# Output projection and first feed-forward blocks of a hybrid GDN layer: earlier row loads, operand preparation in parts, a deferred last tile

## The chip, the cores and the metric

The kernel runs on one core of a Trainium2 chip. The metric is device time in microseconds (us) of one execution, as the median of several runs. Before the change the median of three runs is 2518.31 us (2517.99 to 2518.65). A smaller number is better.

## The reference, cut to what matters

One layer is computed for a prompt of 2048 rows and 128 sample rows, 2176 rows in all, with a width of 1024 and a feed-forward width of 2816 (22 blocks of 128). The change touches the last two lines only:

```
h   = rmsnorm(x);  P = h @ w_in                    # q, k, v, gates, short convolution
o   = gated delta rule(q, k, v, ...);  y = short gated convolution(...)
mix = concat([o, y]) @ w_o
x   = x + rmsnorm(mix, norm_mix_post)
h   = rmsnorm(x, norm_ffn_pre)
x   = x + rmsnorm((silu(h @ w_gate) * (h @ w_up)) @ w_down, norm_ffn_post)
```

## The kernel before, in words

The 2176 rows are 17 tiles of 128 rows, numbered 0 to 16. Every fp32 matrix is split in a high and a low part ("h" and "l" in names such as `xh`, `xl`, `woh`, `wol`), and each product is made of three: high by high, high by low, low by high. The high part is a cast on ScalarE, the low part a subtraction on VectorE or GpSimd.

The program has these stages, by their time in the profiled execution: the projection by `w_in` with convolution and delta rule (0 to about 905 us), the output projection (905 to 1115 us), gate and up products (to about 2010 us) and the down products (to the end). The change lies at the second stage and at its border to the third.

**Output projection.** `o_tile(t)` (line 1022) handles one tile. `o_load` (line 1007) loads the mixer's rows `mr` in two halves (one buffer) and the residual row tile `xo` (two buffers) on SP's queue. `mix_split` (line 983) makes `mh` and `ml` of each half. TensorE then does 48 matmuls of 128x512 (line 1031): 24 for each half of the rows, alternating between two PSUM banks, `dbank` (a pool of 3) and `tbank` (a pool of 2), which hold the two halves of the columns. Behind them stands a chain: squares of the two banks on ScalarE (L1035), their sum on VectorE (`oss`, L1036), the inverse root (`oxm` on VectorE L145, `oxr` by a power on GpSimd L147), scaling on VectorE (L1040), the add into `xo` (L1041), a store to `x2d` on ScalarE's queue, squares of the new rows on ScalarE (L1044), their sum (`oss` L1045), a second inverse root (`oym`, `oyr`), the scaled rows `hx` (L1048, one VectorE instruction of 128x1024), 8 transposes on TensorE into two `ftbank` banks (a pool of 3, L1054), two VectorE multiplications to `ht` (L1055), and a store to `hTd` on ScalarE's queue. `xo` of tile t+2 needs the buffer of tile t, so its load waits for `hx` of tile t.

**Preparing the feed-forward rows.** The feed-forward stage takes the tiles in groups; group 0 holds tiles 0 to 5. Its products follow a Strassen-Winograd scheme of 7 products per block. Seven operands ("parts", in the order B11, T3, T1, T2, B21, T4, B22) are made of blocks of the transposed rows, four column pieces (k = 0 to 3) each: `ffn_load` (line 1141) reads 8 pieces `fh` back from `hTd`, `ffn_sums` (line 1152) makes T3 and T1 on VectorE (L1158, L1159), `ffn_prep` (line 1168) makes T2 (L1175), T4 (L1177) and, for all seven parts, the high cast on ScalarE (L1181) and the low subtraction (L1182), on GpSimd for k = 0 and on VectorE for the others. All that is issued in program order ahead of tiles 8 to 14: with `O_SPLIT` 8, one part ahead of each of the tiles.

**Gate and up blocks.** Block f of a group does seven products of 12 matmuls of 128x384 (L1254) in four PSUM banks (`fbank`, from the same 8 banks in turn: pool `psd` with 3, `pst` with 2, `pft` with 3, and over again). `gu_weights` (line 1203) loads the block's weights `rg` and `ru`, makes four sums (`sA` to `sD`, L1220 to L1223) on VectorE, and splits seven operands `fw`. `gate_up` (line 1277) issues the last three products, fetches the weights of the next block (`ffetch`) and does the elementwise part (`u` L1296, `m` L1297, `c` L1301 to L1303, and so on). Before the first block, weights are fetched and, at its end, the pool for later groups' rows is opened.

**What sets the order.** The program is written as a sequence, and when the kernel is built a scheduler with a modelled timeline puts the instructions of each engine in the order in which they will run. On the chip each engine runs its list in that order. `tc.issue_after(i)` holds what is issued inside it until instruction i is placed.

Of the kernel before, what the change touches and what calls it, by code (L numbers as in the profile page):

```python
# [9 lines left out]
F32 = mybir.dt.float32  # L10
# [3 lines left out]
ALU = mybir.AluOpType  # L14
# [27 lines left out]
        3: (6, 12, 15, 22, 17, 27, 31, 47, (51, 54, 57, 59), 61),  # L42
        4: (6, 12, 15, 20, 17, 24, 29, 42, (45, 48, 50, 52), 55)}
TLS = True
O_SPLIT = 8
NPD, NPT, NPG = 3, 2, 2
NR, NKV, NACC = 3, 2, 3
XKB = 4
# [36 lines left out]
def kernel(  # L85
# [72 lines left out]
    with ExitStack() as ph:  # L158
# [824 lines left out]
        def mix_split(v):  # L983
            mh = oa.tile([P, KD // 2, P], F32R, tag="mh", name="mh", bufs=3)
            ml = oa.tile([P, KD // 2, P], F32R, tag="ml", name="ml", bufs=3)
            A.copy(mh, v)
            V.tensor_sub(ml, v, mh.bitcast(F32))
            return mh, ml
# [28 lines left out]
            nc.sync.dma_start(out=xt, in_=x[t])  # L1017
            return mr, xt

        ahead = []  # L1020

        def o_tile(t):
            mr, xt = ahead.pop() if ahead else o_load(t)
            pss = [psd.tile([P, 512], F32, tag="d", name="dbank"), tbank()]
            for kh in range(2):
                mh, ml = mix_split(mr[kh]) if t else ready_m[kh]
                for j in range(4):
                    k = 4 * kh + j
                    for ci, (m_, w_) in enumerate(((mh, woh), (mh, wol), (ml, woh))):
                        for n in range(2):  # L1030
                            T.matmul(pss[n], m_[:, j, :], w_[k][:, n * 512:(n + 1) * 512],
                                     start=(k == 0 and ci == 0), stop=(k == KD - 1 and ci == 2))
            ss = op.tile([P, 4], F32, tag="oss", name="oss", bufs=2)
            for n in range(2):
                A.activation(ojunk, pss[n], AF.Square, accum_out=ss[:, n:n + 1])  # L1035
            V.tensor_add(ss[:, 0:1], ss[:, 0:1], ss[:, 1:2])  # L1036
            r = rstd(op, ss[:, 0:1], 1, 1.0 / D, EPS, "ox")
            for n in range(2):
                c = slice(n * 512, (n + 1) * 512)
                V.scalar_tensor_tensor(pss[n], pss[n], r, gpost[:, c], op0=ALU.mult, op1=ALU.mult)  # L1040
                V.tensor_add(xt[:, c], xt[:, c], pss[n])  # L1041
            nc.scalar.dma_start(out=x2d[t], in_=xt)
            for n in range(2):
                A.activation(ojunk, xt[:, n * 512:(n + 1) * 512], AF.Square, accum_out=ss[:, 2 + n:3 + n])  # L1044
# [3 lines left out]
            V.tensor_scalar_mul(hx, xt, r)  # L1048
            ht = op.tile([P, KD, P], F32, tag="ht", name="ht") if t else spare[1]
            for n in range(2):  # L1050
                ps = pft.tile([P, 512], F32, tag="t", name="ftbank")
                for q in range(4):
                    k = 4 * n + q
                    T.transpose(ps[:, q * P:(q + 1) * P], hx[:, k * P:(k + 1) * P], ident)  # L1054
                V.tensor_mul(ht[:, 4 * n:4 * n + 4, :], ps.rearrange("p (k c) -> p k c", k=4),  # L1055
                             g_ffn[:, 4 * n:4 * n + 4].unsqueeze(2).broadcast_to([P, 4, P]))
# [5 lines left out]
        ahead.append(o_load(O_SPLIT))  # L1062


    nbank = [0]
# [71 lines left out]
    with ExitStack() as ph:  # L1137
# [14 lines left out]
        def ffn_sums(gi, hs, fs):  # L1152
            hw = len(FGROUPS[gi]) * P // 2
            t3, t2 = [], []
            for k in range(KH):
                b11, b12, b21, b22 = blocks(gi, hs, k)
                t3.append(fs.tile([P, HW], F32, tag="t3", name="ft3", bufs=KH)[:, :hw])
                V.tensor_sub(t3[k], b22, b12)  # L1158
                V.tensor_sub(b12, b12, b11)  # L1159
                if gi:  # L1160
                    t2.append(fs.tile([P, HW], F32, tag="t2", name="ft2", bufs=KH)[:, :hw])
                    V.tensor_sub(t2[k], b22, b12)
                else:
                    t2.append(b12)
            return t3, t2

        def ffn_prep(gi, hs, sums):
            hw = len(FGROUPS[gi]) * P // 2
            t3, t2 = sums
            X = {nm: ([], []) for nm in PARTS}  # L1170
            for nm in PARTS:
                for k in range(KH):
                    b11, b12, b21, b22 = blocks(gi, hs, k)
                    if nm == "T2" and not gi:
                        V.tensor_sub(b12, b22, b12)  # L1175
                    elif nm == "T4":
                        V.tensor_sub(t2[k], b21, t2[k])  # L1177
                    v = {"B11": b11, "B21": b21, "B22": b22, "T3": t3[k], "T1": b12}.get(nm, t2[k])
# [3 lines left out]
                    (G if k == 0 and not gi else V).tensor_tensor(  # L1182
                        out=l[:, :hw], in0=v, in1=h[:, :hw].bitcast(F32), op=ALU.subtract)
# [12 lines left out]
        nw = [0]  # L1196
# [75 lines left out]
        ps_o.close()  # L1272
        side = ExitStack()
        fd = side.enter_context(tc.tile_pool(name="fd", bufs=1, reuse_waits="tile", side="right"))
        ffetch(7 - NWE)

        def gate_up(gi, f, X, banks):
# [56 lines left out]
        for gi in range(len(FGROUPS)):  # L1334
            if gi:
                *_, hid = ffn_prep(gi, hs, t3)
            if gi + 1 < len(FGROUPS):
                hload, hs = ffn_load(gi + 1, fd), []
# [247 lines left out]
```

## Time and profile before

| what | us |
|---|---|
| median of three runs | 2518.31 |
| profiled execution, whole | 2521.97 |
| its span, first to last instruction | 2520.1 |
| TensorE matmuls busy in the span | 2464.6 (98%) |
| VectorE, ScalarE, GpSimd busy | 1612.6, 1063.8, 588.1 |

The profile is of one execution. A line of the timeline has the start in us, the duration in us, the engine, the source line, the operation, what is written and what is read, the shape, and, in brackets, how long the engine had stood idle before it and what ended that. A line of the windows gives for a stretch the length and, for each engine, busy us and instructions, then the granted TensorE clock as a share of full speed, the DMA share and GB/s. PE is TensorE's matmul, PEld its weight load, DVE VectorE, ACT ScalarE, POOL GpSimd, SP the engine that issues loads.

### The profile page before, as it was taken

To read this page: it belongs to the slowest core of one execution; us is meant where nothing else is said; L and a number is where in the kernel's file an instruction comes from. 1 tells how busy PE (TensorE), PEld (TensorE's weight loads), DVE (VectorE), ACT (ScalarE), POOL (GpSimd) and SP (SyncE) were. 2 spreads that over 40 slices of the span, in tenths; PEclk is the share of its full clock that TensorE was granted. 3 is DMA by queue.
4 is the path that set the end of the run, shared out by engine and by line. 5 is a ranking of instruction groups with operands and counts; after the bars stand their busy time and mean duration, and the time that the engine had idled before them with its cause. 6 is when DMAs were issued, how large, how long until landed. Compare 5 with 4: busy or idle time off the path is not lost. (4 is left out here: it accounts for less than half of the span.)

```text
span 2520.1 us, 39370 instructions
## 1 busy us (share of the span) xinstructions
PE 2464.6 (98%) x14366; PEld 2253.3 (89%) x14366; DVE 1612.6 (64%) x3025; ACT 1063.8 (42%) x2355; POOL 588.1 (23%) x663
## 2 busy tenths in 40 slices
PE   8999999999999999999999999999999999999997
PEld 7988888889999988789999999999999987887786
DVE  5966645645666555868878754455555564677688
ACT  5656445445435343534444422223333345333343
POOL 1101011011010001325665400000000055455564
PEclk9999999999999999999999999999999999999999
DMA  7855555456676556669876878878998743344465
GB/s 268 320 205 193 211 194 193 176 181 225 231 243 235 196 187 223 222 227 322 293 273 239 284 246 277 268 246 262 290 308 282 255 146 121 93 126 124 129 222 184
DMA packets 282498, 561.91 MB, mean 223 GB/s; under 512 B 26108, under 2 KB 174784, under 8 KB 265024
## 3 DMA queue, kind: packets, MB, share of 16 engines
q1 hardware_dynamic: 161200, 483.52, 56.6%
q10 hardware_dynamic: 121104, 75.88, 9.6%
q8 instruction: 113, 1.85, 0.3%
q14 instruction: 81, 0.66, 0.1%
HBM read 400.62 MB, written 158.70 MB: 222 GB/s over the span
## 5 line engine op out<-in xcount | busy, mean ns | idle before, releaser
L1254 PE MATMUL fbank<-xh,fw 128*128 128x384 f32 (+1 forms) x3696 | 898.9, 326 | 4.5 <-DVE ht L1055 2.0
L298 PE MATMUL dbank<-hi,w 128*128 128x384 f32 (+1 forms) x2240 | 671.9, 368 | 8.9 <-ACT w L277 6.0
L1254 PEld LDWEIGHTS fbank<-xh,fw 128*128 128x128 f32 x3696 | 651.9, 188 | 5.8 <-ACT m L1290 2.6
L1254 PE MATMUL fbank<-xl,fw 128*128 128x384 f32 (+1 forms) x1848 | 602.5, 326 | 0.0
L298 PEld LDWEIGHTS dbank<-hi,w 128*128 128x128 f32 x2240 | 416.7, 190 | 48.2 <-ACT w L277 6.2
L1418 PE MATMUL fbank<-dw,as 128*128 128x512 f32 x1884 | 445.2, 395 | 8.0 <-DVE as L1402 2.8
L1418 PEld LDWEIGHTS fbank<-dw,as 128*128 128x128 f32 x1884 | 355.2, 189 | 91.8 <-DVE acc L1377 4.1
L298 PE MATMUL dbank<-lo,w 128*128 128x384 f32 (+1 forms) x1120 | 402.2, 359 | 1.1 <-DVE lo L216 1.1
L1254 PEld LDWEIGHTS fbank<-xl,fw 128*128 128x128 f32 x1848 | 347.4, 188 | 0.0
L1402 POOL TENSOR_TENSOR as<-ar,as 128x256 fp32r<-128x256 f32 (+1 forms) x207 | 186.4, 911 | 230.1 <-ACT as L1399 227.0
L298 PEld LDWEIGHTS dbank<-lo,w 128*128 128x128 f32 x1120 | 212.9, 190 | 18.7 <-DVE lo L216 1.6
L1377 DVE TENSOR_TENSOR acc<-acc,fbank 128x512 f32<-128x512 f32 x248 | 166.3, 682 | 97.5 <-PE fbank L1418 83.4
L1399 ACT CAST as<-ar 128x256 fp32r<-128x256 f32 (+1 forms) x288 | 118.6, 427 | 187.1 <-PE fbank L1418 133.8
L1110 POOL TENSOR_TENSOR dw<-dr,dw 128x512 fp32r<-128x512 f32 x48 | 70.2, 1473 | 521.5 <-ACT dw L1108 521.4
L1229 ACT CAST fw<-rg 128x512 fp32r<-128x512 f32 x124 | 77.3, 623 | 187.8 <-PE fbank L1254 158.9
L302 DVE SCALAR_TENSOR_TENSOR acc<-R,cw,acc 128x384 f32<-128x384 f32 (+2 forms) x180 | 121.6, 677 | 53.0 <-ACT acc L332 44.4
L1301 DVE TENSOR_TENSOR c<-u,fbank 128x384 f32<-128x384 f32 (+1 forms) x66 | 34.9, 529 | 116.0 <-PE fbank L1254 116.0
L1299 ACT ACTIVATE m<-fbank 128x384 f32<-128x384 f32 (+1 forms) x66 | 31.3, 474 | 132.8 <-PE fbank L1254 131.8
L1297 DVE TENSOR_TENSOR m<-m,m 128x384 f32<-128x384 f32 (+1 forms) x44 | 23.1, 525 | 92.1 <-ACT m L1290 92.0
L1230 POOL TENSOR_TENSOR fw<-rg,fw 128x512 fp32r<-128x512 f32 x44 | 68.6, 1558 | 45.0 <-ACT fw L1229 44.8
L324 POOL COPY hist<-R 128x3 f32<-128x3 f32 x60 | 18.3, 305 | 255.1 <-ACT R L307 202.1
L1290 ACT COPY m<-fbank 128x384 f32<-128x384 f32 (+1 forms) x66 | 30.5, 461 | 88.5 <-PE fbank L1254 57.0
(362 smaller groups left out, 3573.6 us busy)
## 6 DMA issues: line engine op xcount, KB each, us to landing
w<-wsplit SPq DMA_DIRECT2D x105, 1024.0 KB, 5.1
fw<-fsplit SPq DMA_DIRECT2D x188, 512.0 KB, 4.6
fsplit<-fw SPq DMA_DIRECT2D x94, 512.0 KB, 3.9
partd<-pt ACTq DMA_DIRECT2D x88, 384.0 KB, 6.3
rg<-in_w_gu SPq DMA_DIRECT2D x62, 512.0 KB, 3.6
wsplit<-w SPq DMA_DIRECT2D x28, 1024.0 KB, 4.9
ar<-partd SPq DMA_DIRECT2D x48, 384.0 KB, 3.3
wr<-in_w_in SPq DMA_DIRECT2D x34, 512.0 KB, 5.9
```

The costliest lines, as they stand in the source:

```text
L298: T.matmul(ps[:, :c], l[:, k, :], r[k][:, :c], start=(k == 0 and r is hi and l is wh), stop=(k == KD - 1 and l is wl))
L302: r = V.scalar_tensor_tensor(acc, raw(d), w[:, d:d + 1], acc, op0=ALU.mult, op1=ALU.add)
L1110: e.tensor_tensor(out=w[1], in0=v, in1=w[0].bitcast(F32), op=ALU.subtract)
L1229: A.copy(w[:, 0], v)
L1230: e.tensor_tensor(out=w[:, 1], in0=v, in1=w[:, 0].bitcast(F32), op=ALU.subtract)
L1254: T.matmul(ps, w_[:, c], b_[k][:, :hw], start=(first and k == 0 and ci == 0), stop=(k == KH - 1 and ci == 2), skip_group_check=not first)
L1299: A.activation(sg0, b1, AF.Silu)
L1301: V.tensor_add(c21, u2, b3)
L1377: V.tensor_add(dst, dst, ps)
L1399: ins = A.copy(a[:, 0, :n], v)
L1402: e.tensor_tensor(out=a[:, 1, :n], in0=v, in1=a[:, 0, :n].bitcast(F32), op=ALU.subtract)
L1418: T.matmul(ps, a[:, x_, q * P:(q + 1) * P], w[y_], start=(start and q == 0 and ci == 0), stop=(q == c - 1 and ci == 2), skip_group_check=True)
```

## The change

Five edits:

1. **Rows a tile ahead.** `o_load(t+1)` is issued inside `o_tile(t)`, behind the two row splits of tile t and ahead of its matmuls.
2. **`o_tile` in two.** The second half (squares, scaling, transposes, store) becomes `o_rows`. For the last tile it is deferred until the first gate/up block has been issued; only then are the output projection's pools closed and the later groups' pool `fd` opened. The loads of group 1 begin at block 3's code instead of ahead of block 0 (each is still issued where it was, from block 4).
3. **Preparation part by part.** The loads start a tile earlier (`O_SPLIT` 7), four ahead of tile 7 and four behind. The sums T3, T1 and T2 are made inside their part, four column pieces at a time, and each part is issued behind the second-norm squares and the last add of the tile before it.
4. **k = 0 subtractions** of group 0 go from GpSimd to VectorE.
5. **Bank order.** `fbank` takes the eight banks in the order `pft`, `pst`, `psd` instead of `psd`, `pst`, `pft`.

```diff
-O_SPLIT = 8
+O_SPLIT = 7
...
-        ahead = []
+        rows_in, omark = {0: o_load(0)}, {}
         def o_tile(t):
-            mr, xt = ahead.pop() if ahead else o_load(t)
+            mr, xt = rows_in.pop(t)
+            halves_m = [mix_split(mr[kh]) if t else ready_m[kh] for kh in range(2)]
+            if t + 1 < NT:
+                rows_in[t + 1] = o_load(t + 1)
...
-                V.tensor_add(xt[:, c], xt[:, c], pss[n])
+                omark["V"] = V.tensor_add(xt[:, c], xt[:, c], pss[n])
             nc.scalar.dma_start(out=x2d[t], in_=xt)
+            if t + 1 < NT:
+                o_rows(t, xt, ss)
+            else:
+                omark["last"] = lambda: o_rows(t, xt, ss)
+
+        def o_rows(t, xt, ss):
...
-        pool, tag = (psd, "d") if i < NPD else (pst, "t") if i < NPD + NPT else (pft, "t")
+        pool, tag = (pft, "t") if i < 8 - NPD - NPT else (pst, "t") if i < 8 - NPD else (psd, "d")
...
-                    if nm == "T2" and not gi:
+                    if nm == "T3" and not sums:
+                        t3.append(fs.tile([P, HW], F32, tag="t3", name="ft3", bufs=KH)[:, :hw])
+                        V.tensor_sub(t3[k], b22, b12)
+                    elif nm == "T1" and not sums:
+                        V.tensor_sub(b12, b12, b11)
+                    elif nm == "T2" and not sums:
                         V.tensor_sub(b12, b22, b12)
...
-                    (G if k == 0 and not gi else V).tensor_tensor(
-                        out=l[:, :hw], in0=v, in1=h[:, :hw].bitcast(F32), op=ALU.subtract)
+                    V.tensor_sub(l[:, :hw], v, h[:, :hw].bitcast(F32))
...
-            hs = list(ffn_load(0, fs))
-            prep = ffn_prep(0, hs, ffn_sums(0, hs, fs))
-            for t in range(O_SPLIT, O_SPLIT + len(PARTS)):
-                hid = next(prep)
-                o_tile(t)
+            hload = ffn_load(0, fs)
+            hs = [next(hload) for _ in range(KH)]
+            o_tile(O_SPLIT)
+            hs += hload
+            prep = ffn_prep(0, hs, fs=fs)
+            for i in range(len(PARTS)):
+                with tc.issue_after(omark["A"].ins), tc.issue_after(omark["V"].ins):
+                    hid = next(prep)
+                if i + 1 < len(PARTS):
+                    o_tile(O_SPLIT + 1 + i)
...
+                if (gi, f) == (0, 0):
+                    omark["last"]()
+                    ps_o.close()
+                    fd = side.enter_context(tc.tile_pool(name="fd", bufs=1, reuse_waits="tile", side="right"))
+                if f == 3 and gi + 1 < len(FGROUPS):
+                    hload, hs = ffn_load(gi + 1, fd), []
```

What the built programs do with it is shown at two places, both on VectorE; in these rows "x2" or "x4" is a row that stands so many times. The first place is the end of tile 7's chain and the start of tile 8's: `oym` and `hx` are tile 7's, the `oss` sum behind `hx` is tile 8's, and `xl`, `fh`, `ft` are preparation. Before:

```order
L145 TENSOR_SCALAR oym<-oss 128x1
L1182 TENSOR_TENSOR xl<-fh,xh 128x384
L1159 TENSOR_TENSOR fh<-fh 128x384
L1182 TENSOR_TENSOR xl<-fh,xh 128x384
L1175 TENSOR_TENSOR fh<-fh 128x384
L1182 TENSOR_TENSOR xl<-ft_10205,xh 128x384
L1182 TENSOR_TENSOR xl<-fh,xh 128x384
L1182 TENSOR_TENSOR xl<-ft_10208,xh 128x384
L1048 TENSOR_SCALAR hx<-xo,oyr 128x1024
L1182 TENSOR_TENSOR xl<-fh,xh 128x384
L1036 TENSOR_TENSOR oss<-oss 128x1
```

The same place after the change, where L1054, L1057, L1039, L1043 and L1192 are the lines that were L1045, L1048, L1036, L1040 and L1182:

```order
L1054 TENSOR_TENSOR oss<-oss 128x1
L145 TENSOR_SCALAR oym<-oss 128x1
L1192 TENSOR_TENSOR xl<-fh,xh 128x384 x2
L1057 TENSOR_SCALAR hx<-xo,oyr 128x1024
L1192 TENSOR_TENSOR xl<-fh,xh 128x384 x2
L1039 TENSOR_TENSOR oss<-oss 128x1
L145 TENSOR_SCALAR oxm<-oss 128x1
L1043 SCALAR_TENSOR_TENSOR dbank<-dbank,oxr,gpost 128x512
L1043 SCALAR_TENSOR_TENSOR tbank<-tbank,oxr,gpost 128x512
```

Seven preparation instructions of several parts stood between `oym` and `hx`; now two of one part stand there, and the four of that part are all there is between tile 7's `oym` and tile 8's `oss`.

The second place is the border between the stages: `hx` and `ht` are tile 16's, `c_11408` and `c_11381` are the first of the two elementwise sums of gate/up block 0 that release its banks. Before:

```order
L1301 TENSOR_TENSOR c_11408<-u_11403,fbank 128x384
L1045 TENSOR_TENSOR oss<-oss 128x1
L145 TENSOR_SCALAR oym<-oss 128x1
L1230 TENSOR_TENSOR fw<-sD,fw 128x512
L1048 TENSOR_SCALAR hx<-xo,oyr 128x1024
L1220 TENSOR_TENSOR sC<-rg,ru 128x512
L1221 TENSOR_TENSOR sA<-ru 128x512
L1222 TENSOR_TENSOR sB<-sA,rg 128x512
L1230 TENSOR_TENSOR fw<-sC,fw 128x512
L1223 TENSOR_TENSOR sD<-rg,sB 128x512
L1316 TENSOR_TENSOR a_11414<-c_11408,m_11406 128x384
L1055 TENSOR_TENSOR ht<-ftbank,vec 128x512 x2
```

After:

```order
L1244 TENSOR_TENSOR fw<-sB,fw 128x512
L1054 TENSOR_TENSOR oss<-oss 128x1
L145 TENSOR_SCALAR oym<-oss 128x1
L1244 TENSOR_TENSOR fw<-sD,fw 128x512
L1057 TENSOR_SCALAR hx<-xo,oyr 128x1024
L1313 TENSOR_TENSOR c_11381<-u_11376,fbank 128x384
L1234 TENSOR_TENSOR sC<-rg,ru 128x512
L1235 TENSOR_TENSOR sA<-ru 128x512
```

The sum `c` has gone from ahead of `oss` to behind `hx`; the two `ht` rows stand seven rows further on. On TensorE tile 16's transposes stand 93 matmuls of the gate/up blocks behind the output projection's last matmul, where they stood 86 behind it; tile 7's stand 12 matmuls into tile 9's 48, where they stood 2 matmuls into tile 10's, and those of tiles 8 to 14 stand 14 or 23 or 24 matmuls into the tile two further on.

More of the change, by code (lines that the diff above doesn't have):

```diff
@@ L1018, in o_load @@
             return mr, xt
-        ahead = []
+        rows_in, omark = {0: o_load(0)}, {}
         def o_tile(t):
-            mr, xt = ahead.pop() if ahead else o_load(t)
+            mr, xt = rows_in.pop(t)
+            halves_m = [mix_split(mr[kh]) if t else ready_m[kh] for kh in range(2)]
+            if t + 1 < NT:
+                rows_in[t + 1] = o_load(t + 1)
             pss = [psd.tile([P, 512], F32, tag="d", name="dbank"), tbank()]
             for kh in range(2):
-                mh, ml = mix_split(mr[kh]) if t else ready_m[kh]
+                mh, ml = halves_m[kh]
                 for j in range(4):
@@ L1061 @@
             o_tile(t)
-        ahead.append(o_load(O_SPLIT))
     nbank = [0]
@@ L1159, in ffn_sums, with ffn_prep @@
                 V.tensor_sub(b12, b12, b11)
[L1160 to L1164, printed above, removed]
+                t2.append(fs.tile([P, HW], F32, tag="t2", name="ft2", bufs=KH)[:, :hw])
+                V.tensor_sub(t2[k], b22, b12)
             return t3, t2
-        def ffn_prep(gi, hs, sums):
+        def ffn_prep(gi, hs, sums=None, fs=None):
             hw = len(FGROUPS[gi]) * P // 2
-            t3, t2 = sums
+            t3, t2 = sums or ([], [blocks(gi, hs, k)[1] for k in range(KH)])
             X = {nm: ([], []) for nm in PARTS}
@@ L1177, in ffn_prep @@
                         V.tensor_sub(t2[k], b21, t2[k])
-                    v = {"B11": b11, "B21": b21, "B22": b22, "T3": t3[k], "T1": b12}.get(nm, t2[k])
+                    v = t3[k] if nm == "T3" else {"B11": b11, "B21": b21, "B22": b22, "T1": b12}.get(nm, t2[k])
                     h = fp.tile([P, HW], F32R, tag=f"xh{nm}{k}", name="xh")
@@ L1271 @@
         fb = ph.enter_context(tc.tile_pool(name="fb", bufs=1, reuse_waits="tile"))
-        ps_o.close()
         side = ExitStack()
-        fd = side.enter_context(tc.tile_pool(name="fd", bufs=1, reuse_waits="tile", side="right"))
         ffetch(7 - NWE)
```

4 lines of the change are left out of this document (1 added, 3 removed).

## Prediction

> **What bounds the kernel now.** I read the page first, then windows of the stages, then the waits of PE between 890 and 1160 us, and last the timeline around them. The page's busy line and two windows:
>
> ```profile
> PE 2464.6 (98%) x14366; PEld 2253.3 (89%) x14366; DVE 1612.6 (64%) x3025; ACT 1063.8 (42%) x2355; POOL 588.1 (23%) x663
> ...
> 960.00:980.00 20.00, 20.00 (x98) 16.75 (x97) 9.33 (x20) 5.76 (x15) 2.20 (x4) 1.00 0.62 185
> ...
> 1020.00:1040.00 20.00, 13.88 (x53) 10.64 (x52) 17.87 (x38) 8.14 (x19) 7.43 (x6) 0.84 0.43 147
> 1130.00:1140.00 10.00, 6.74 (x42) 6.13 (x40) 9.88 (x9) 3.04 (x6) 7.34 (x6) 1.00 1.00 377
> 1200.00:1920.00 720.00, 717.68 (x4292) 717.04 (x4291) 445.96 (x716) 254.38 (x517) 138.79 (x96) 1.00 0.82 271
> ```
>
> PE is the bound: 98% busy, in the gate/up stage 717.68 of 720. So only a gap in PE's work can be won or lost. Two stretches that the change touches are not full: 1020 to 1040 (13.88 of 20, at a clock of 0.84) and 1130 to 1140 (6.74 of 10). In both DVE is full instead (17.87 of 20, 9.88 of 10), while in an ordinary stretch of the same stage it has 9.33 of 20. PE's waits in 890 to 1160 say for whom:
>
> ```profile
> PE dbank L1031 <- DVE xo L1041: 4.4, 1, 4.4
> PE ftbank L1054 <- DVE hx L1048: 3.0, 2, 1.8
> PE fbank L1254 <- DVE ht L1055: 2.0, 1, 2.0
> ```
>
> All three are DVE's, and the timeline of PE (start, duration) places them:
>
> ```profile
> 1010.95 0.39 PE L1031 MATMUL dbank<-woh,mh 128*128 128x512 f32 x1
> ...
> 1021.83 0.39 PE L1031 MATMUL dbank<-woh,mh 128*128 128x512 f32 x1
> 1022.05 0.39 PE L1031 MATMUL dbank<-wol,mh 128*128 128x512 f32 x1
> ...
> 1024.19 1.07 PE L1054 MATMUL ftbank<-cst,hx 128*128 128x128 f32 x8 [1.75 <-DVE hx L1048]
> ...
> 1034.93 0.77 PE L1031 MATMUL dbank<-woh,mh 128*128 128x512 f32 x1 [4.37 <-DVE xo L1041]
> ...
> 1091.15 0.39 PE L1031 MATMUL dbank<-woh,mh 128*128 128x512 f32 x1
> ...
> 1102.93 0.39 PE L1031 MATMUL dbank<-woh,mh 128*128 128x512 f32 x1
> ...
> 1114.71 0.33 PE L1254 MATMUL fbank<-xh,fw 128*128 128x384 f32 x1
> ...
> 1130.38 0.34 PE L1254 MATMUL fbank<-xl,fw 128*128 128x384 f32 x1
> 1131.99 1.06 PE L1054 MATMUL ftbank<-cst,hx 128*128 128x128 f32 x8 [1.27 <-DVE hx L1048]
> ...
> 1137.41 0.51 PE L1254 MATMUL fbank<-xh,fw 128*128 128x384 f32 x2
> 1139.90 0.44 PE L1254 MATMUL fbank<-xh,fw 128*128 128x384 f32 x1 [1.99 <-DVE ht L1055]
> ```
>
> 1010.95 and 1021.83 are the first matmuls of tiles 9 and 10, 1091.15 and 1102.93 those of tiles 15 and 16, 1114.71 the first of gate/up block 0. Why DVE is late shows on its timeline and on GpSimd's:
>
> ```profile
> 1009.11 1.38 DVE L1158 TENSOR_TENSOR ft<-fh 128x384 f32<-128x384 f32 x1
> ...
> 1013.12 0.55 DVE L1159 TENSOR_TENSOR fh<-fh 128x384 f32<-128x384 f32 x1
> ...
> 1022.57 1.48 DVE L1048 TENSOR_SCALAR hx<-xo,oyr 128x1024 f32<-128x1024 f32 x1 [0.45 <-POOL oyr L147]
> ...
> 1034.70 0.68 DVE L1041 TENSOR_TENSOR xo<-xo,tbank 128x512 f32<-128x512 f32 x1
> ```
> ```profile
> 1018.99 3.55 POOL L147 TENSOR_TENSOR oyr<-oym,neghalf 128x1 f32<-128x1 f32 x1 [3.50 <-DVE oym L145]
> ...
> 1088.56 0.55 POOL L147 TENSOR_TENSOR oyr<-oym,neghalf 128x1 f32<-128x1 f32 x1 [4.29 <-DVE oym L145]
> ```
>
> From 1009 on, DVE's list holds the preparation of all seven parts ahead of `hx` of tile 7; the two engines also hold each other up: GpSimd's power takes 3.55 here and 0.55 later, a DVE sum 1.38 here and 0.55 a little later. `hx` of tile 7 comes at 1022.57, and the load of `xo` for tile 9, which waits for it, leaves SP's queue only then:
>
> ```profile
> 1024.11 0.33 SPq L1017 DMA_DIRECT2D xo<-in_x  x1
> ```
>
> The last add of tile 8, behind more preparation, ends at 1034.70 + 0.68 = 1035.4; PE's wait of 4.37 is for that chain.
>
> **The change part by part.**
>
> **Middle (parts, loads ahead, k = 0 subtractions).** From the start of tile 9 to the end of tile 16 PE takes 1114.71 - 1010.95 = 103.76, for 8 tiles and 8 sets of transposes. A tile with one set and no wait takes 1102.93 - 1091.15 = 11.78; eight are 94.2. The loss is 9.5. Of it 1.75 and 4.37 are the two waits, and a good part of the rest is a slow clock behind the second:
>
> ```profile
> 1034.90:1040.60 5.70, 5.67 (x13) 4.46 (x14) 4.46 (x12) 3.09 (x9) 1.28 (x2) 0.50 0.98 346
> ```
>
> 5.70 at a clock of 0.50 is 2.85 lost; 0.5 is left over.
>
> Whether the loss goes depends on when each tile's `hx` is ready against when PE needs it. The chain without preparation, tile 14's:
>
> ```profile
> 1100.62 0.75 DVE L1048 TENSOR_SCALAR hx<-xo,oyr 128x1024 f32<-128x1024 f32 x1 [0.73 <-POOL oyr L147]
> ```
>
> From the tile's last matmul (1091.15, where the next begins) to 1101.37 is 10.2. The part issued between adds at most 8 DVE instructions (4 sums, 4 subtractions) ahead of `hx`: 8 x 0.55 = 4.4, so 14.6. PE's list asks for it 23 matmuls into the tile after next, at 11.78 + 23 x 0.227 = 17.0 (0.227 is 11.78 less 0.9 for eight transposes, over 48): 2.4 spare. Where PE asks earlier, less stands ahead: tile 7 (12 in, 14.5) has two subtractions, 11.3; tiles 11 and 13 (14 in, 15.0) four, 12.4. Per tile, DVE's work is 9.33/20 x 11.78 = 5.5, with a part 9.9 of 11.78: it keeps up, but only just. The seven k = 0 subtractions are in that count; on GpSimd they cost 1.1 each by the row of its group:
>
> ```profile
> L1182 POOL TENSOR_TENSOR xl<-fh,xh x6: 985/1105/1336, 1002.8 to 1029.5; 128x384 fp32r<-128x384 f32 x6
> ```
>
> The 28 high casts are as many as before, on an engine that is 5.76 of 20 busy. So I take back the whole 9.5.
>
> Here a rule can be weighed. The row is the power of 3.55 us beside a queue of DVE sums of 0.55. The Trainium skill, "SBUF — State Buffer", section "SBUF: two separate sides", says that a two-input DVE operation and a GpSimd operation share a port pair as a lock, taken by whichever starts first and held for its whole instruction. By that the power should wait for one sum, about 0.55, and not for 3.0 more than its own 0.55, so the measurement decides. With two to four preparation instructions near `oym` now, the rule would add at most 0.55 to a chain and the row at most 2.2; both lie inside the 2.4 spare, so the sum is the same.
>
> Loads a tile ahead: `mr` has one buffer, so a load still waits for the low split of the tile before; it lands in 3.6, against 11.78 a tile. I cost it at nothing; without that cover it would be 3.6 once a tile, and SP's queue would show it.
>
> ```profile
> mr<-mixo SPq DMA_DIRECT2D x8, 256.0 KB, 3.6
> ...
> ru<-in_w_gu SPq DMA_DIRECT2D x2, 512.0 KB, 6.2
> ```
>
> The weights `rg`, `ru` of block 0 now stand behind `mr` of tile 16 in that queue, and six VectorE instructions on them stand ahead of tile 14's `hx`. At 0.68 (the add of 128x512 above) they make 10.2 + 4.1 = 14.3; at the 1.21 that one took beside GpSimd, 17.5, which is 0.5 too late:
>
> ```profile
> L1220 DVE TENSOR_TENSOR sC<-rg,ru 128x512 f32<-128x512 f32 x1 | 1.2, 1206 | 0.0
> ```
>
> I take 15 to 16.5, and nothing for it; the upper end goes to a rival.
>
> **Border (deferred last rows, bank order).** 1130.38 to 1131.99 is 1.61 in place of one matmul's 0.17 (717.68/4292): 1.44. 1137.41 to 1139.90 is 2.49 in place of 0.35: 2.14. Together 3.6. Rows of DVE there:
>
> ```profile
> 1128.25 0.54 DVE L1301 TENSOR_TENSOR c<-u,fbank 128x384 f32<-128x384 f32 x1
> ...
> 1130.09 1.76 DVE L1048 TENSOR_SCALAR hx<-xo,oyr 128x1024 f32<-128x1024 f32 x1 [0.44 <-POOL oyr L147]
> ```
>
> `hx` of tile 16 ends at 1131.85, 17.1 behind the end of tile 16. With `c` (0.54) put behind it, 16.6. PE now comes to those transposes after 93 block matmuls in place of 86. The 86 took 1130.38 + 0.17 - 1114.71 = 15.85 with tile 15's transposes between, so 93 take 17.0: just late enough. But the second half of the transposes goes into a bank that `c` must read first: 16.6 + 0.54 = 17.1, asked for at 17.0 + 0.45. The second wait, on `ht`, came because block 1 used the banks that the transposes had; by the new bank order it uses the other pools, so it goes. That stall's successor would be block 2, which comes some 25 us later. I allow 1.0 for the narrow margin at the transposes.
>
> **Sum.** -9.5 - 3.6 + 1.0 = -12.1. The profiled execution is 2521.97 (span 2520.1 and 1.87 around it), 3.66 above the median of three, so it becomes 2509.9, and the median 2518.31 - 12.1 = 2506.2. All the order outside 1000 to 1150 us is the same, so nothing else is counted.
>
> **The rivals.**
>
> *The border's waits stay.* DVE is 9.88 of 10 busy there and `hx` ran at 1.76 in place of 0.75 beside a full GpSimd:
>
> ```profile
> 1130.50:1132.00 1.50, 0.23 (x3) 0.04 (x1) 1.50 (x2) 0.00 (x0) 1.50 (x2) 1.00 1.02 415
> ```
>
> If the chain slips a little more, tile 16's transposes wait as before: -9.5, 2508.8. Chance 0.13.
>
> *One or two chains of the middle are late*, tile 14's first (17.5 against 17.0, or a late landing of `ru`). Each would cost a wait like 1.75 and perhaps a slow clock behind it. What a short wait can do is seen elsewhere:
>
> ```profile
> 1398.07 0.44 PE L1254 MATMUL fbank<-xh,fw 128*128 128x384 f32 x1 [1.77 <-ACT m L1290]
> ```
> ```profile
> 1398.98:1402.39 3.41, 3.41 (x13) 3.41 (x12) 3.38 (x4) 1.59 (x4) 3.41 (x4) 0.50 0.86 301
> ```
>
> Behind 1.77 of waiting stood 3.41 at half clock, 1.7 lost; behind the 1.27 and 1.99 at the border the window 1130 to 1140 has 1.00. So a late chain costs 1.75 to 3.5: 2508.0 to 2509.7 for one, up to 2513.2 for two. Chance 0.08. The Trainium skill, "TensorE: Matmul & The Clock Gate", Part 1, has the clock halve only after an idle window of about 3.4 us. The 4.37 above agrees, the 1.77 does not, so the measurement decides; by the page alone two late chains would end at 2509.7.
>
> *No gain.* What is won in the middle is waited for again at the border or in the blocks. Against it: PE is the bound behind it, 717.68 of 720, with no slack that would absorb an earlier start. 2518, chance 0.04.
>
> *Slower: the parts are slow as they were in places before.* If the preparation on DVE runs at 1.38 (the row at 1009.11) and not at 0.55, each chain is 10.2 + 8 x 1.38 = 21.2 against 17.0: 4.2 late and a slow clock of 1.7, for six tiles 35, less the 13.1: about 2540. It decides from (17.0 - 10.2)/8 = 0.85 per instruction. The groups of 1000 to 1045 (count, busy us, mean ns) speak for it and against it:
>
> ```profile
> L1182 DVE TENSOR_TENSOR xl<-fh,xh 128x384 fp32r<-128x384 f32 x18 | 10.6, 593 | 0.0
> ...
> L1158 DVE TENSOR_TENSOR ft<-fh 128x384 f32<-128x384 f32 x4 | 3.8, 958 | 0.0
> ```
>
> The four sums with a mean of 958 stood beside GpSimd subtractions, which are gone; eighteen others have 593. Chance 0.05.
>
> **How the numbers follow.** The forecast, 2506.2, has 0.70; its own range is 2503.5 to 2509: below, if the allowance isn't needed (2505.2) and the unprofiled runs lose 1.7 more than I read; above, if the border's gain is mostly missed. The border rival (0.13) lies in or beside it. The range is widened to the two late chains, 2513, which leaves no more than 2 in 10 out with what my sizes may miss. A change under about 0.2%, 5 us, can't be told from none. Faster (2513.3 or less): 0.70 + 0.13 + 0.08 = 0.91, less a little, 0.90; same 0.05; slower 0.05.
>
> **What would show it.** Right: PE full in the 20 us windows between 1010 and 1110, no wait on `xo` or `hx` there, the clock at 1.00, GpSimd's power near 0.55 throughout, tile 16's last matmul about 9.5 earlier against tile 9's first, and no wait on `ht` behind it. Wrong: DVE sums of over 0.85 between tiles 8 and 14, a wait of PE for `hx` at tile 14, or for `hx` or `c` at tile 16.

## The result, and the profile after

The changed kernel takes 2509.27 us (median of 6 runs, 2506.84 to 2511.47) where the kernel before takes 2518.45 (6 runs, 2517.99 to 2519.84): a ratio of 0.996, 95% interval 0.995 to 0.997, so 7.6 to 12.6 us faster. Forecast was 2506.2, in a range of 2503.5 to 2513.0. The profiled execution after took 2506.84, with a span of 2505.1.

PE's waits between 890 and 1160 us, after the change:

```profile
PE fbank L1268 <- ACT m L1301: 1.4, 2, 1.2
PE dbank L1034 <- ACT mh L986: 1.3, 1, 1.3
PE dbank L1034 <- DVE wol L1001: 0.4, 1, 0.4
PE ftbank L1063 <- DVE hx L1057: 0.2, 1, 0.2
```

The waits for `xo` (4.4) and `ht` (2.0) are gone, that for `hx` has fallen from 3.0 to 0.2. Rows two and three lie in tile 0 and were there before. Row one is new: PE waits for a copy `m` of ScalarE. The windows of the two stretches, of which the second, the border, now begins 10.4 us earlier (1104.33 in place of 1114.71):

```profile
1020.00:1040.00 20.00, 20.00 (x98) 16.72 (x98) 14.66 (x33) 7.53 (x20) 2.38 (x4) 1.00 0.52 170
...
1120.00:1130.00 10.00, 9.77 (x60) 9.47 (x59) 9.89 (x12) 3.79 (x7) 7.11 (x6) 1.00 1.03 407
1130.00:1140.00 10.00, 9.80 (x57) 9.49 (x56) 9.90 (x12) 4.78 (x9) 7.57 (x6) 1.00 1.02 373
1140.00:1150.00 10.00, 8.83 (x51) 8.51 (x50) 6.18 (x9) 3.31 (x7) 2.65 (x3) 1.00 1.02 336
```

The middle is full, at a clock of 1.00, with DVE at 14.66 of 20 in place of 17.87. At the border PE has small gaps; the largest is in 1140 to 1150, where DVE is not full and ScalarE has only 3.31. PE's timeline:

```profile
1010.09 0.39 PE L1034 MATMUL dbank<-woh,mh 128*128 128x512 f32 x1
...
1104.33 0.33 PE L1268 MATMUL fbank<-xh,fw 128*128 128x384 f32 x1
...
1121.74 1.06 PE L1063 MATMUL ftbank<-cst,hx 128*128 128x128 f32 x8 [0.23 <-DVE hx L1057]
...
1147.86 0.44 PE L1268 MATMUL fbank<-xh,fw 128*128 128x384 f32 x1 [1.17 <-ACT m L1301]
```

Tiles 9 to 16 take 1104.33 - 1010.09 = 94.24, to the hundredth eight times 11.78. Tile 16's transposes wait 0.23.

The next table cuts PE's timeline of each profiled execution into stages. A gate/up block has 84 matmuls (7 products of 12), so blocks 0 to 3 run from the first block matmul to the 337th, blocks 4 to 15 to the 1345th and blocks 16 to 18 to the 1597th. At the border the built order can put some products of the next block ahead of this one's last, so a cut is one by count. The last column runs from the start of the last of all block matmuls to the end of the span. In us:

| kernel | tiles 9 to 16 | blocks 0 to 3 | blocks 4 to 15 | blocks 16 to 18 | behind the last gate/up matmul | median, ratio to before (95%) |
|---|---|---|---|---|---|---|
| before | 103.76 | 64.28 | 174.72 | 47.65 | 483.4 | 2518.45, 1 |
| after | 94.24 | 62.37 | 175.03 | 48.81 | 479.6 | 2509.27, 0.996 (0.995 to 0.997) |
| after, once more | 94.24 | 62.60 | 174.95 | 48.77 | 483.1 | 2510.77, 0.9957 (0.9944 to 0.9970) |
| parts only | 94.24 | 66.14 | 174.72 | 46.38 | 481.7 | 2511.59, 0.9960 (0.9948 to 0.9973) |
| border only | 103.75 | 63.70 | 175.20 | 48.59 | 479.9 | 2521.43, 1.0002 (0.9993 to 1.0010) |
| parts not held | 96.14 | 63.53 | 175.05 | 47.14 | 482.6 | 2513.80, 0.9971 (0.9961 to 0.9981) |
| old bank order | 94.24 | 64.37 | 175.50 | 48.96 | 481.0 | 2512.30, 0.9961 (0.9948 to 0.9975) |
| last tile not deferred | 94.24 | 68.31 | 174.72 | 48.65 | 482.8 | 2516.92, 0.9987 (0.9977 to 0.9996) |
| k = 0 on GpSimd | 96.35 | 64.97 | 176.43 | 46.50 | 480.3 | 2513.88, 0.9971 (0.9959 to 0.9982) |
| low subtractions doubled | 94.24 | 64.15 | 175.33 | 48.83 | 481.9 | 2514.12, 0.9972 (0.9961 to 0.9983) |
| sums of group 1 spread | 94.24 | 62.99 | 174.85 | 46.02 | 485.4 | 2512.76, 0.9967 (0.9955 to 0.9980) |
| stores on SP | 94.24 | 60.91 | 174.72 | 44.27 | 482.3 | 2505.28, 0.9938 (0.9925 to 0.9950) |
| before, stores on SP | 102.31 | 63.81 | 174.72 | 44.22 | 479.5 | 2516.18, 0.9982 (0.9974 to 0.9991) |
| both on SP and spread | 94.24 | 60.94 | 174.72 | 43.68 | 482.9 | 2504.50, 0.9932 (0.9920 to 0.9945) |

Each ratio is to runs of the kernel before on the same chip; the kernel before had medians of 2518.45, 2520.28, 2520.22 and 2521.14 on the chips used, so the ratios are to be compared. Between the traces of before and after the change is -9.52 in the middle, -1.91 in blocks 0 to 3, +0.31 in blocks 4 to 15 and +1.16 in blocks 16 to 18: -9.96 in these stages, 0.996 of the profiled execution before. The two profiled executions are 15.1 apart; the rest lies ahead of tile 9 (1010.95 against 1010.09), in the blocks behind block 18 (0.5) and mostly in the down products (483.4 against 479.6). That last column runs from 479.5 to 485.4 over these traces, and the same kernel has 479.6 and 483.1 in two executions, so a difference of that size there is not put down to an edit.

### The profile page after: what moved, and what is told of

It reads as the page before. It is cut to its first block, busy times and chain, and to the rows that moved or that the text cites. A ratio compares the mean times of both kernels' runs of the same rounds, so it can differ in the third digit from the quotient of the medians.

```text
span 2505.1 us, 39369 instructions
## 1 busy us (share of the span) xinstructions
PE 2455.0 (98%) x14366; PEld 2247.2 (90%) x14366; DVE 1610.7 (64%) x3032; ACT 1059.6 (42%) x2355; POOL 579.5 (23%) x656
```

## The experiments

**The changed kernel once more.** No edit.

> The changed kernel once more, for a second trace and more times. Theory A (what is saved lies in the middle, 9.5 us, and at the border, 2.3 us, and both are the same in every execution; the executions differ by waits and half-clock stretches further on): tiles 9 to 16 take 94.2 us again and blocks 0 to 3 take 62 to 63 us, while the whole lies anywhere from 2506.5 to 2511.5 us. Rival C (the first trace was a lucky one, and the saving in these two places varies itself): the 94.2 or the 62.2 grows by 2 us or more where the whole is longer.

The middle is the same to the hundredth and the border to 0.23 us, in an execution that took 2512.41, 5.6 longer. Theory A held for the two places, and Rival C is out. What differs lies elsewhere, though not all further on as Theory A had it: 3.5 in the last column and 2.0 ahead of tile 9, which begins at 1012.08 in place of 1010.09.

**The parts alone.** The changed kernel without its three other edits:

```diff
-            mr, xt = rows_in.pop(t)
+            mr, xt = o_load(t)
...
-            if t + 1 < NT:
-                o_rows(t, xt, ss)
-            else:
-                omark["last"] = lambda: o_rows(t, xt, ss)
+            o_rows(t, xt, ss)
...
-        pool, tag = (pft, "t") if i < 8 - NPD - NPT else (pst, "t") if i < 8 - NPD else (psd, "d")
+        pool, tag = (psd, "d") if i < NPD else (pst, "t") if i < NPD + NPT else (pft, "t")
...
```

> Only the preparation part by part, held behind the marks, with the k = 0 subtractions on VectorE; row loads, last tile and bank order as before the change. Theory A: tiles 9 to 16 take 94.2 us, blocks 0 to 3 take 64.5 us as before the change (PE waits for hx and ht of tile 16), the whole is 7 to 9.5 us below the kernel before, 2509 to 2511.5 us. Rival B (a part of the middle's gain comes from the loads a tile ahead): tiles 9 to 16 take 96 us or more.

94.24: the parts, with the k = 0 move, give all of the middle's gain, the loads a tile ahead none of it. (From tile 0's first matmul to block 0 the traces of this kernel and of the changed one have the same instructions in the same order on every engine, but for one load of `xo`: on SP it stands behind four loads of `fh` in the changed kernel and behind eight here.) PE's waits of this kernel from 1005 to 1175:

```profile
PE fbank L1262 <- DVE ht L1058: 2.0, 1, 2.0
PE ftbank L1057 <- DVE hx L1051: 1.3, 1, 1.3
PE fbank L1262 <- DVE xo L1041: 0.5, 1, 0.5
```

The two waits of the border are those from before the change, as expected. But blocks 0 to 3 take 66.14, not 64.5: behind the wait for `ht` the clock stands at half, which costs 1.7, and the wait for `xo` is new.

```profile
1132.40:1135.81 3.41, 3.41 (x13) 3.41 (x12) 2.79 (x5) 1.96 (x4) 1.28 (x1) 0.50 1.02 390
```

By its ratio of 0.9960 this kernel can't be told from the whole change (0.996 and 0.9957). What the two border edits bring is shown in the stages only.

**The border alone.** The kernel before with the deferral and the new bank order (its preparation and loads untouched).

```diff
+            if t + 1 < NT:
+                o_rows(t, xt, ss)
+            else:
+                omark["last"] = lambda: o_rows(t, xt, ss)
...
+        pool, tag = (pft, "t") if i < 8 - NPD - NPT else (pst, "t") if i < 8 - NPD else (psd, "d")
...
+                if (gi, f) == (0, 0):
+                    omark["last"]()
...
```

> Only the last tile's deferred rows and the bank order; preparation and loads as before the change. Theory A: tiles 9 to 16 take 103.8 us as before the change, blocks 0 to 3 take about 62.2 us instead of 64.5 us, the whole 2516 us (1.5 to 3 us below the kernel before). Rival (the border's loss only moves to the next wait): 2518 us, no difference.

Blocks 0 to 3 gain 0.6, not 2.3, and the whole nothing (1.0002): the rival was right. PE's waits between 1005 and 1175 us say where the gain went:

```profile
PE dbank L1031 <- DVE xo L1041: 4.4, 1, 4.4
PE fbank L1260 <- ACT m L1293: 2.7, 2, 1.4
PE ftbank L1060 <- DVE hx L1054: 2.0, 2, 1.8
```

`ht` is gone, and of the 2.0 for `hx` 1.8 is tile 7's in the middle. In their place PE waits twice for ScalarE's copy `m`, 1.30 in block 1 and 1.39 in block 2. That made ScalarE the question.

**The parts not held.**

```diff
             for i in range(len(PARTS)):
-                with tc.issue_after(omark["A"].ins), tc.issue_after(omark["V"].ins):
-                    hid = next(prep)
+                hid = next(prep)
```

> The changed kernel with the parts no longer held behind the last add and the squares of the tile before; GpSimd still has none of the subtractions. The built order again puts the preparation of several parts ahead of tile 7's scaled rows. Theory A (the pile of preparation in VectorE's order is the cause): PE again waits for hx of tile 7 or the adds of tile 8, tiles 9 to 16 take 98 to 104 us, the whole 2512 to 2518 us. Rival D (GpSimd and VectorE holding each other up is the cause, and it went with the k = 0 subtractions): tiles 9 to 16 take under 95.5 us and the whole is as the changed kernel, 2507 to 2511 us.

96.14, with one wait of 1.61 for tile 8's add: between the two theories, since Theory A had 98 to 104 and Rival D under 95.5. The pile stood there again, with `hx` of tile 7 at 1021.55, but without GpSimd's subtractions its low subtractions ran at a mean of 552, and the clock stayed at 1.00 behind the wait. So taking out the hold alone costs 1.9 of the 9.5.

**The old bank order, and the last tile not deferred,** each in the changed kernel.

```diff
-        pool, tag = (pft, "t") if i < 8 - NPD - NPT else (pst, "t") if i < 8 - NPD else (psd, "d")
+        pool, tag = (psd, "d") if i < NPD else (pst, "t") if i < NPD + NPT else (pft, "t")
```

> The changed kernel with the old bank order; the last tile's rows still deferred. In the built order tile 16's transposes are back at 86 block matmuls and the first sum c is back ahead of its oss. Theory A (the bank order removes the wait for ht, and it, not the deferral, sets where the transposes stand): PE waits again for hx of tile 16 (about 1.3 us) and for ht (about 2.0 us), blocks 0 to 3 take 64.5 to 66.3 us, tiles 9 to 16 stay at 94.2 us; the whole is within 2 us of the kernel with the parts alone. Rival (the deferral does the work): blocks 0 to 3 take 62.5 us and there is no wait for ht.

Blocks 0 to 3 took 64.37, where the kernel before has 64.28; PE waited 1.34 for `hx` and 1.97 for `ht`, so Theory A held: without the bank order the deferral brings nothing. (The parts alone have almost the same two waits and take 66.14. The clock there fell to half behind them; here the window 1120 to 1140 has 1.00.)

```diff
-            if t + 1 < NT:
-                o_rows(t, xt, ss)
-            else:
-                omark["last"] = lambda: o_rows(t, xt, ss)
+            o_rows(t, xt, ss)
...
-                    omark["last"]()
...
```

> The changed kernel with tile 16's rows not deferred; the new bank order stays. In the built order the transposes of tile 16 stand 48 block matmuls in, where PE is about 9 us behind the end of tile 16, and hx of tile 16 cannot be there before 13 to 16 us. Theory A: PE waits 3 to 6 us for hx of tile 16, perhaps with a half-clock stretch behind it; blocks 0 to 3 take 65 to 70 us, 3 to 7 us more than in the changed kernel. Rival (the deferral is without effect, the bank order does all): 62.5 us.

68.31, 5.9 more, as expected in size; but the cause was another. PE's timeline, with tile 15's transposes first and tile 16's last, and two rows of ScalarE:

```profile
1105.10 1.03 PE L1060 MATMUL ftbank<-cst,hx 128*128 128x128 f32 x8
...
1111.06 0.45 PE L1265 MATMUL fbank<-xh,fw 128*128 128x384 f32 x1 [3.88 <-ACT fw L1240]
...
1113.38 1.01 PE L1265 MATMUL fbank<-xh,fw 128*128 128x384 f32 x2 [0.98 <-POOL fw L1241]
...
1121.54 1.04 PE L1060 MATMUL ftbank<-cst,hx 128*128 128x128 f32 x8
```
```profile
1105.69 0.62 ACT L1240 CAST fw<-sD 128x512 fp32r<-128x512 f32 x1
...
1110.39 0.62 ACT L1240 CAST fw<-sC 128x512 fp32r<-128x512 f32 x1 [2.08 <-DVE sC L1231]
```

The transposes of tile 16 wait for nothing; PE waits for weights. The cast at 1105.69 is the last of block 0's, and the one at 1110.39, which ends the wait of 3.88, is one of block 1's: after 12 block matmuls PE already wants weights of block 1 that aren't split yet. Behind it the clock stands at 0.50 from 1112.01 to 1118.84. That the built order comes to this because, with tile 16's rows ahead of block 0 in the program, block 0's banks have to come behind them is my reading and not shown. The bank order and the deferral work only together.

**k = 0 on GpSimd,** in the changed kernel:

```diff
-                    V.tensor_sub(l[:, :hw], v, h[:, :hw].bitcast(F32))
+                    (G if k == 0 and not gi else V).tensor_tensor(
+                        out=l[:, :hw], in0=v, in1=h[:, :hw].bitcast(F32), op=ALU.subtract)
```

> The changed kernel with the seven k = 0 subtractions back on GpSimd. Theory A (the pile on VectorE was the cause; one GpSimd subtraction beside four VectorE instructions costs a chain 1 to 3 us, and the built order asks for hx 4 to 8 matmuls earlier): tiles 9 to 16 take 94.2 to 96 us, the power on GpSimd is late by 1 to 2 us in places, the whole is within 2 us of the changed kernel. Rival D (the collision was the cause): waits of PE for hx and tiles 9 to 16 of 98 us or more.

96.35, just over what Theory A gave, with waits ahead of the transposes of tile 12 (1.02, for `hx`) and of tile 14 (0.66, put down to `oss`); blocks 0 to 3 lost 2.6 as well, with a wait of 1.29 for `ht`, and the whole lost some 3 (0.9971), where Theory A had 2 at most. On GpSimd six of these subtractions took a mean of 1264, on VectorE 551. Taking the move back costs 2.1 in the middle; Rival D's 98 wasn't reached.

**The low subtractions doubled.** Each of the 28 for group 0 is made twice; the values stay the same.

```diff
-                    V.tensor_sub(l[:, :hw], v, h[:, :hw].bitcast(F32))
+                    for _ in range(1 if gi else 2):
+                        V.tensor_sub(l[:, :hw], v, h[:, :hw].bitcast(F32))
```

> The changed kernel with each low subtraction of group 0 done twice, 28 instructions of about 0.55 us more on VectorE between tiles 7 and 14. It measures how near the preparation is to where it would cost time. Theory A (VectorE has 9.9 of 11.78 us per tile, so four more make 12.1, just over): tiles 9 to 16 take 94.2 to 98 us, with waits of PE for hx or xo of 0 to 2 us late in the stretch; the rival of the prediction in which slow preparation costs 4.2 us and a slow clock for each of six tiles would give 110 us or more.

In the middle nothing is lost: 94.24. The window 1010 to 1105 of the changed kernel and of this one:

```profile
1010.00:1105.00 95.00, 95.00 (x454) 79.46 (x453) 71.86 (x150) 42.82 (x109) 11.93 (x18) 1.00 0.65 217
```
```profile
1010.00:1105.00 95.00, 95.00 (x453) 79.37 (x452) 86.91 (x182) 44.15 (x112) 19.37 (x18) 1.00 0.64 213
```

DVE had 71.86 of 95 and now has 86.91, still under; the built order puts the transposes later (those of tiles 9 and 10 stand 39 and 44 matmuls into the tile two further on, not 24 and 23). Blocks 0 to 3 lose 1.6 to 1.8: PE waits 1.28 and 1.38 for `m` there, where the changed kernel has 0.20 and 1.17. Why the first of these grew stays open. The ratio of 0.9972 overlaps the changed kernel's.

**Group 1's sums spread,** in the changed kernel, as the change does it for group 0 (`ffn_sums` takes the two lists and the pieces to make):

```diff
...
-                    if f == NF - 6:
+                    if f == 12:
+                        t3 = ([], [])
+                    if 12 <= f < 12 + 2 * KH and f % 2 == 0:
                         with tc.issue_after(gmark["V"].ins):
-                            t3 = ffn_sums(gi + 1, hs, fd)
+                            ffn_sums(gi + 1, hs, fd, *t3, [(f - 12) // 2])
```

> The changed kernel, with group 1's sums (12 VectorE instructions in one pile behind block 16) spread over blocks 12, 14, 16 and 18, three instructions each: the same treatment as the change gives to group 0. Theory E (the loss of 2.7 to 5.4 us at blocks 16 to 18 is that pile, which delays c and with it the copies on ScalarE): blocks 16 to 18 take 43.7 to 44.5 us in place of 46.4 to 49.1, the whole is 3 to 5 us below the changed kernel, about 2506 us where that has 2510. Rival F (the loss is the issue of the partd stores on ScalarE's queue, which stand ahead of the copies): the loss stays, 47 us or more.

Blocks 16 to 18 took 46.02, 2.8 less than in the changed kernel: neither Theory E's 43.7 to 44.5 nor Rival F's 47 or more. The whole is not faster (0.9967 against 0.9957, intervals that overlap). Waits for `m` came up later (0.65 and 0.58 at 1415 and 1445).

**The stores on SP,** in the changed kernel, both lines that store to `partd`:

```diff
-                    nc.scalar.dma_start(out=partd[gi][ch][j, :, 1:7, q, :], in_=pt[:, :, j * P:(j + 1) * P])
+                    nc.sync.dma_start(out=partd[gi][ch][j, :, 1:7, q, :], in_=pt[:, :, j * P:(j + 1) * P])
...
-                nc.scalar.dma_start(out=partd[gi][ch][:, :, 0, q, :].rearrange("j p c -> p j c"),
+                nc.sync.dma_start(out=partd[gi][ch][:, :, 0, q, :].rearrange("j p c -> p j c"),
```

> The changed kernel with the partd stores of the gate/up blocks issued on SP's queue in place of ScalarE's. Rival F (ScalarE stands behind these stores, which wait for VectorE and take 2 us to issue, and its copies come late): the waits on m at 1148 us (1.2) and at blocks 16 to 18 (2.7 and 1.9) go or halve, blocks 0 to 3 take about 61 us, blocks 16 to 18 under 46 us, the whole 3 us or more below the changed kernel. Theory E (VectorE's pile): the wait at L1300, which comes ahead of the stores, stays at 2.7 us and the whole gains 2 us at most; it loses if the weight loads on SP now stand behind stores that wait.

Rival F was right: blocks 0 to 3 take 60.91, blocks 16 to 18 44.27, and the whole 2505.28 (0.9938). ScalarE of the changed kernel around the wait at 1147.86:

```profile
1142.16 0.62 ACT L1243 CAST fw<-ru 128x512 fp32r<-128x512 f32 x1
1145.34 1.90 ACTq L1340 DMA_DIRECT2D partd<-pt  x3
1147.33 0.48 ACT L1301 COPY m<-fbank 128x384 f32<-128x384 f32 x1 [4.54 <-PE fbank L1268]
```

ScalarE stands still from 1142.8 to 1147.3: first until VectorE has made the last `pt`, at 1145.30 by its row, then 1.90 for three stores.

```profile
1144.74 0.56 DVE L1338 TENSOR_TENSOR pt<-pt 128x384 f32<-128x384 f32 x1
```

The releaser that the row names, PE, had been done; what held the copy was the queue ahead of it. With the stores on SP:

```profile
1142.68 0.62 ACT L1243 CAST fw<-ru 128x512 fp32r<-128x512 f32 x1
1143.20 0.48 ACT L1301 COPY m<-fbank 128x384 f32<-128x384 f32 x1
```

The copy follows at once. The stores go out on SP at 1146.55, and the load of `ru` behind them at 1148.54; PE has no wait over 0.2 from there to 1378. Theory E's claim that the wait at L1300 stays at 2.7 fell too: at 1378 it is 0.31. But a wait of 1.18 for L1300 comes at 1394, in block 19, which takes 16.04 in place of 14.56. So of the 4.5 gained in blocks 16 to 18, 1.5 is lost in the next block, and the whole gate/up stage gains 4.8 (916.26 for 921.09).

**The kernel before with the stores on SP.** The same two lines.

> The kernel before, with nothing changed but the partd stores of the gate/up blocks on SP's queue. Theory F (the stores on ScalarE's queue, not the change, set what is lost at blocks 16 to 18, and they gave back a part of the change's gain): tiles 9 to 16 take 103.8 us, blocks 0 to 3 take 64 to 64.5 us (the waits for hx and ht of tile 16 stay), blocks 16 to 18 about 44.3 us; the whole 3 to 5 us below the kernel before. The changed kernel with the stores on SP is then about 13 us faster than this one (9.5 of the middle and 3.4 at the border), which is the whole of what I called recoverable. Rival (the stores on SP are worth their gain only behind the change): no difference to the kernel before, and a distance of 15 us.

Blocks 16 to 18: 44.22, as expected; the waits at the border stay (1.29 and 1.98); the whole is 0.9982, 4.5 us under the kernel before. With the stores on SP on both sides, the change gives 0.9938 / 0.9982 = 0.9956, 11.1 us; in the traces 102.31 - 94.24 = 8.1 in the middle and 63.81 - 60.91 = 2.9 at the border, 11.0 together. So the expectation's 13 was 2 too much: 1.1 because the slow clock behind the wait of 4.39 was shorter in this execution (below), 0.4 because the wait for `hx` of tile 7 was 1.34 and not 1.75, and 0.5 at the border.

**Both.** Stores on SP and group 1's sums spread.

> The changed kernel with both: partd stores on SP, and group 1's sums spread over blocks 12 to 18. Theory F (the stores were the cause, the pile of sums only its trigger): blocks 16 to 18 take 43.7 to 44.3 us and the whole is as with the stores on SP alone, within 1 us. Theory E (both cost): 1 to 2 us below it. It is the version that should be the fastest of all, 2504 to 2506 us where the kernel before has 2520.

2504.50, 0.9932 (0.9920 to 0.9945): the fastest of all, some 6 to 7 us under the changed kernel by the ratios, though not to be told from the stores alone. Blocks 16 to 18 take 43.68, three times the 14.56 of an undisturbed block (174.72 / 12); block 19 takes 16.31, and the gate/up stage 915.98, only 0.3 less than with the stores alone. That fits Theory F, that the stores were the cause and the pile of sums its trigger. By the medians the difference to Theory E is too small to decide.

## Why the prediction was right, and where it was off

- **Middle, -9.5: right in size and mechanism; the hundredth is luck.** The steady tile of 11.78 times eight was the right measure of what the changed kernel takes, 94.24 in every trace that keeps the parts held and the k = 0 move. What the kernel before takes varies with its slow clock: 103.76 in one execution, and 102.31 with the stores on SP, where the same sum gives 8.1. The chains: `hx` of tile 9, with four sums and four subtractions ahead, was done 1036.71 + 0.76 - 1021.87 = 15.6 behind its tile (1021.87 is 1010.09 + 11.78), where I had 14.6, and PE asked at 17.2; 1.6 was to spare, not 2.4. Tile 14, the rival's weak place, was done 12.7 behind its tile, where I had taken 15 to 16.5.

```profile
1036.71 0.76 DVE L1057 TENSOR_SCALAR hx<-xo,oyr 128x1024 f32<-128x1024 f32 x1 [0.73 <-POOL oyr L147]
1039.10 1.03 PE L1063 MATMUL ftbank<-cst,hx 128*128 128x128 f32 x8
```

- **Prices of the preparation: right.** All ran at 546 to 553, and the low subtractions at:

```profile
L1192 DVE TENSOR_TENSOR xl<-fh,xh 128x384 fp32r<-128x384 f32 x24 | 12.0, 551 | 0.1
```

  GpSimd's power `oyr` fell from a mean of 986 to 647. The rival of slow parts (over 0.85) didn't come. Its threshold was not tested: with the subtractions doubled nothing is lost in the middle, but there the built order moves the transposes back with them, which it would not do for instructions that are slower only on the chip.
- **Which edit does it: I had counted the three as one.** The loads ahead bring nothing in the middle. Taking out the hold alone costs 1.9 and taking back the move of k = 0 alone 2.1. How the other 5.5 splits between the remaining edits (sums inside the parts, loads of `fh` a tile earlier) and the working together of all was not tried.
- **Border, -3.6 + 1.0 = -2.6: the two waits went as said, but the gain was 0.7 to 0.9 smaller** (62.37 and 62.60 for 64.28). The transposes' margin was narrow as said: PE waits 0.23 and 0.36 for `hx` of tile 16, one of the signs of being wrong, at a size that costs little. The step that failed is the one behind the second wait, "That stall's successor would be block 2, which comes some 25 us later". It asks only when the transposes' banks are used again. PE did stop in block 2, 1.17 at 1147.86, but for ScalarE's copy `m`, held up by the partd stores on its queue. I had named what VectorE and PE would be late for and not what ScalarE's list holds. The allowance of 1.0 was made for the transposes and went mostly to this other wait; that it was nearly enough is luck. With the stores on SP the border gives 2.9 to 3.4, most of the 3.6.
- **The border's base.** The sum adds the border's gain to the middle's as if blocks 0 to 3 took the same with the parts alone as before. With the parts alone they took 66.14, since the clock fell to half there. Against that the border edits bring 3.8; against the old bank order, which has the same two waits without the slow clock, 1.8 to 2.0.
- **Outside, nothing: off by 1.4.** Blocks 4 to 18 took 1.5 more in the first trace and 1.35 in the second, with the same pile of group 1's sums and the same stores there. Blocks 16 to 18 run from 46.4 to 49.0 over the kernels that have both, so it isn't shown that the change costs this.
- **The sum:** -12.1 was forecast. In these stages it was -10.0, by the medians -9.2 and by the second chip's ratio 0.9957, -10.8.

## What to carry to other kernels

Where PE waits for an engine that is in the middle of prefetched preparation, look at that engine's order, and issue the preparation in portions that fit beside one tile; measure the gain against an undisturbed tile. Then look along every in-order list that the freed work passes, the DMA issues on a compute engine's queue too: a store that waits for another engine holds all that stands behind it. Compare stages in the trace before the whole, since here the last stage differed by 3.5 us between two executions of the same kernel. And look where a gain in one stage goes: here waits for one engine gave way to waits for another.

## What the runs showed of the hardware

- **The slow clock behind a wait varies, here in steps of 3.41 us.** Around the same wait for tile 8's add (4.37, 4.41 and 4.39 in three executions) the clock stood at half for different times. In the order kernel before, border alone, kernel before with the stores on SP:

```profile
1033.75:1040.57 6.82, 5.64 (x13) 4.46 (x14) 5.58 (x14) 3.61 (x10) 1.28 (x2) 0.50 0.88 307
```
```profile
1033.45:1040.27 6.82, 5.52 (x13) 4.39 (x14) 5.58 (x14) 3.63 (x10) 1.28 (x2) 0.50 0.87 297
```
```profile
1034.52:1037.93 3.41, 3.41 (x10) 2.65 (x9) 2.90 (x8) 2.61 (x9) 0.73 (x1) 0.50 0.97 329
1037.94:1041.00 3.06, 3.06 (x15) 2.46 (x14) 2.15 (x4) 0.00 (x0) 0.55 (x1) 1.00 0.97 363
```

  Two stretches are twice 3.41 and begin inside the wait; the third is 3.41 and begins 0.47 behind its end. The tiles took 103.76, 103.75 and 102.31. The stretch at the border with the parts alone is 3.41 as well, and the same two waits left the clock at 1.00 with the old bank order. The Trainium skill, "TensorE: Matmul & The Clock Gate", Part 1, says that the window in which activity is counted runs freely, so that one kernel can show different numbers of slow matmuls at its start; the stretches here, in mid-kernel, agree with a window of that kind.
- **A GpSimd power was slow beside an unbroken row of VectorE work, with no other GpSimd work near it.** With the parts not held, GpSimd had stood idle for 12.15 when the power `oyr` of tile 7 began. VectorE ran preparation back to back from 1017.13 to 1020.01, and the power took 3.08; a later one took 0.55:

```profile
1017.36 3.08 POOL L147 TENSOR_TENSOR oyr<-oym,neghalf 128x1 f32<-128x1 f32 x1 [12.15 <-DVE oym L145]
...
1053.98 0.55 POOL L147 TENSOR_TENSOR oyr<-oym,neghalf 128x1 f32<-128x1 f32 x1 [4.77 <-DVE oym L145]
```

  In the changed kernel, where two subtractions at most stand between `oym` and `hx`, the nine powers `oyr` from 1000 to 1105 us took 0.55 to 0.88.
